# Down-projection of the feed-forward: earlier first operands, a longer last group, sums of weights by DMA

## The chip, the cores and the metric

The kernel runs on one core of a Trainium2 chip. The metric is the device time of one execution in microseconds (us), lower is better; the time of a kernel is the median of its runs.

The engines are TensorE (PE; PEld is its loading of weights), VectorE (DVE), ScalarE (ACT), GpSimd (POOL) and SyncE (SP), which issues most transfers. SBUF is the on-chip memory that all engines read; products of TensorE land in banks of PSUM. Each engine works through its own queue in order and waits there for what others have to deliver.

## What is computed

A trunk of two layers over 512 positions of width 1024, in float32. Each layer is a mixer (attention of three kinds, not touched here), a feed-forward of inner width 2816, and a gated embedding, with layer norms between:

```python
x = layer_norm(alpha * x + mixer(x))
x = layer_norm(alpha * x + swiglu(x, w1, w3, w2))
x = x + sigmoid(x @ w_gate + b_gate) * (p[i] @ w_proj)

def swiglu(x, w1, w3, w2):
    return (jax.nn.silu(x @ w1) * (x @ w3)) @ w2
```

## The kernel before

**Numbers in two parts.** A float32 operand is split into a rounded part (`whi`, `bh`; ScalarE copies it into type fp32r) and the rest (`wlo`, `bl`; VectorE or GpSimd subtracts). `mm3` makes three matmuls of a product: part by rest, part by part, rest by part. `wload` (L137) does it for weights: SyncE loads halves of 128x512 into `wraw` (3 buffers), ScalarE rounds, and a rotation picks the engine for the rest; `DENSE` (L131) gives two of three to VectorE and one to GpSimd. Weight pieces live in 4 buffers `hi` and 4 `lo`.

**The feed-forward** (`swiglu`, L652) has 22 tiles of 128 rows of the inner width. `up` (L656) makes one tile: 8 products by w1 and 8 by w3, in all 48 matmuls of 512 columns (`ps_h`, two banks), then silu on ScalarE and the product on VectorE. The first 16 tiles go in 4 groups of 4 (`GROUPS`). A group's down-projection (`down`, L687) is a product of matrices cut into 2x2 blocks with seven block products in place of eight, on sums and differences of blocks: `B[k][i]` are blocks of the hidden tiles (`halves`, buffers of tag `pl`), `W(j, k)` blocks of w2 (`w2raw`, buffers of tag `qk`, of which there are 3), `n1` to `n4` differences of B, `s3` and `s1` sums of W. `operands(m)` (L715) makes product m's operands and splits them; the loop of L745 asks for those of m+1 and then makes product m with 12 matmuls, 6 for each of two banks `ps_m`. The products are added into x or into four accumulators (`sums`).

**The order.** `down` is a generator with one step for each product. It is made after a group's four `up`s, but nothing of it is issued until it is first asked, which is after the first `up` of the next group; `after_up(2)` then takes two steps after each `up`. Steps of the fourth group lie among the tiles that are left: tiles 16 to 21 (`plain`), which go in pairs. Tile 16 is followed by three steps, tile 17 by the rest and by `flush` (L767), which puts the accumulators into x with six operations of VectorE and three of GpSimd. Pairs are kept as parts in `gT` (a `qk` buffer for each pair) and multiplied by rows of w2 in `down_pair` (L781), 48 matmuls a pair; the last pair is done in `finish`, where the norm and the gate follow tile by tile.

All instructions of the kernel are placed by a planner that simulates the engines: the order of the code is a priority, and what is ready in its simulation may go ahead if buffers are free. The result is one fixed order on each engine.

Of the kernel before, what the change touches and what calls it, by code (L numbers as in the profile page):

```python
# [8 lines left out]
F32 = mybir.dt.float32  # L9
F32R = mybir.dt.float32r  # L10
# [4 lines left out]
P = 128  # L15
LINE = 32
S = 512
# [32 lines left out]
def trunk(ctx: ExitStack, tc: tile.TileContext, a, out):  # L50
# [81 lines left out]
    STICK = (acts, dve), (gps,)  # L132
    MLA = (acts, dve), (gps,)
    FOX = (acts,), (gps,)
    engines, count = [DENSE], [0]

    def wload(src, n, m):  # L137
# [512 lines left out]


    def swiglu(i, finish):  # L652
        w1, w3, w2 = a["ffn_w1"][i], a["ffn_w3"][i], a["ffn_w2"][i]
        nf = DFF // P

        def up(f, g, cuts=1):  # L656
# [30 lines left out]
        def down(f0, halves):  # L687

            first = f0 == 0
            raw = []
            for p in range(2):
                t = quad("w2raw", F32)
                nc.sync.dma_start(t.rearrange("p (k j) c -> p k (j c)", k=2),  # L700
                                  w2[(f0 + 2 * p) * P:(f0 + 2 * p + 2) * P, :].rearrange("(k p) c -> p k c", k=2))
                raw.append(t)
            B = [[halves[i][:, :, k, :] for i in range(2)] for k in range(2)]

            def W(j, k):
                return [t[:, 2 * k + j, :] for t in raw]

            s3, s1 = ([wide(n)[:, q * S:(q + 1) * S] for q in range(2)] for n in ("s3", "s1"))
            n1, n2, n3, n4 = (temp(n).rearrange("p (q s) -> p q s", q=2) for n in ("n1", "n2", "n3", "n4"))

            def add(o, a, b, eng):
                for q in range(2):
                    eng[q].tensor_tensor(o[q], a[q], b[q], ALU.add)

            def operands(m):  # L715
                tt = dve.tensor_tensor
                ws, bs = [(W(0, 1), B[1][0]), (W(0, 0), B[0][0]), (s3, n3), (s1, n1), (s1, n2), (W(1, 1), n4),
                          (s1, B[1][1])][m]
                if m == 2:
                    add(s3, W(0, 0), W(1, 0), (dve, gps))  # L720
                    tt(n3, B[0][1], B[1][1], ALU.subtract)
                elif m == 3:
                    add(s1, W(1, 0), W(1, 1), (dve, gps))
                    tt(n1, B[0][0], B[0][1], ALU.subtract)
                elif m == 4:
                    add(s1, s1, W(0, 0), (dve, gps))
                    dve.scalar_tensor_tensor(n2, B[1][1], -1.0, n1, ALU.mult, ALU.subtract)
                elif m == 5:
                    tt(n4, n2, B[1][0], ALU.add)
                elif m == 6:  # L730
                    add(s1, s1, W(0, 1), (dve, gps))
                parts = act.tile([P, 2, S], F32R, tag="g", bufs=3, name="bparts")
                bh, bl = (parts[:, c, :].rearrange("p (q s) -> p q s", q=2) for c in range(2))
                acts.copy(bh, bs)
                dve.tensor_tensor(bl, bs, bh.bitcast(F32), ALU.subtract)
                hi = wpool.tile([P, D], F32R, tag="hi", name="whi")
                lo = wpool.tile([P, D], F32R, tag="lo", name="wlo")
                wh, wl = ([v[:, q * S:(q + 1) * S] for q in range(2)] for v in (hi, lo))
                for q in range(2):
                    acts.copy(wh[q], ws[q])  # L740
                    (dve, gps)[(q + m) % 2].tensor_tensor(wl[q], ws[q], wh[q].bitcast(F32), ALU.subtract)  # L741
                return (bh, bl), (wh, wl)

            ready = operands(0)
            for m in range(7):  # L745
                (bs, ws), ready = ready, operands(m + 1) if m < 6 else None
                for tb in range(2):
                    ps = (ps_pq, ps_o)[tb]("ps_m")
                    for q in range(2):
                        mm3(ps, both(bs, lambda v: v[:, q, blk(tb)]), both(ws, lambda v: v[q]), q == 0, q == 1)  # L750
                    if m in (0, 5, 6):
                        o = x[tb + 2 * (m == 6)][:, (m == 5) * S:(m == 5) * S + S]
                        if first:
                            dve.scalar_tensor_tensor(o, o, ALPHA, ps, ALU.mult, ALU.add)
                        else:
                            dve.tensor_tensor(o, o, ps, ALU.add)
                    else:
                        if first and tb == 0:
                            sums[m] = row_tile("acc").rearrange("p (t c) -> p t c", t=2)
                        o = sums[m][:, tb, :]  # L760
                        if first:
                            acts.copy(o, ps)
                        else:
                            dve.tensor_tensor(o, o, ps, ALU.add)
                yield

        def flush():  # L767

            q1, q7, p5, p6 = (sums[m] for m in (1, 2, 3, 4))
            h00, h01, h10, h11 = (x_rows[:, 2 * i:2 * i + 2, j * S:(j + 1) * S] for j in range(2) for i in range(2))  # L770
            dve.tensor_tensor(p6, q1, p6, ALU.add)
            gps.tensor_tensor(h00, h00, q1, ALU.add)
            dve.tensor_tensor(h10, h10, q7, ALU.add)
            dve.tensor_tensor(q7, q7, p5, ALU.subtract)
            gps.tensor_tensor(h01, h01, p5, ALU.add)
            dve.scalar_tensor_tensor(h11, h11, ALPHA, q7, ALU.mult, ALU.add)
            dve.tensor_tensor(h10, h10, p6, ALU.subtract)
            gps.tensor_tensor(h01, h01, p6, ALU.add)
            dve.tensor_tensor(h11, h11, p6, ALU.subtract)
# [14 lines left out]
        for f0 in range(0, 4 * GROUPS, 4):  # L794
            halves = [spare("gb").rearrange("p (q k s) -> p q k s", q=2, k=2) for _ in range(2)]
            for n in range(4):
                up(f0 + n, as_block(halves, n // 2, n % 2), 2 if f0 + n == 0 else 1)
                after_up(2)
            after_up(7)
            steps = down(f0, halves)  # L800
        waiting = None
        for f in range(nf - plain, nf, 2):
            group = quad("gT")
            gs = [(group[:, 2 * j, :], group[:, 2 * j + 1, :]) for j in range(2)]
            for j in range(2):
                up(f + j, as_parts(gs[j]))
                if f == nf - plain:
                    after_up(3)
            if waiting is None:
                after_up(7)  # L810
                flush()
            else:
                down_pair(*waiting)
            waiting = (f, gs)
        finish(gs, row_weights(w2, [nf - 2, nf - 1]))


# [295 lines left out]
    for i in range(DEPTH):  # L1113
# [12 lines left out]

        def finish(gs, w):
            first_half, rest = gate(i, e, a["w_gate"][i], done)
            finish_rows(gs, w, False, norm_params("ln2_g", "ln2_b"), after=first_half)
            rest()  # L1130

# [104 lines left out]
```

## Time and profile before

| | |
|---|---|
| median of 3 runs | 1392.12 us (1392.1 to 1394.07) |
| the profiled execution | 1396.08 us |
| its span, first to last instruction | 1394.4 us |
| PE busy | 1346.4 us, 97% |
| DVE, ACT, POOL busy | 925.9, 659.9, 534.1 us |
| mean granted TensorE clock | 0.986 |
| moved by DMA | 131.74 MB, mean 94 GB/s |

The profile is of one execution. A row of the view by line groups instructions of one line, engine and operation; the number behind the bar `|` is the busy time of the group and the mean time of one, then the idle time of that engine just ahead of them and what ended it. A row in order of time has the start, the time taken (of several merged ones, from the first to the last end), and in brackets the idle time ahead of it and what ended that. `out<-in` are the program's names. Matmuls are pipelined: one takes longer than the distance to the next, so their pace is read from the starts. In the feed-forward the first layer's stage lies from some 286 to 640 us, the second's from 975 to 1330.

### The profile page before, as it was taken

Reading aid. Unit: us, or ns where it says so; the run is one execution under the profiler, and the core shown is the slowest. Engines: PE = TensorE matmul, PEld = TensorE weight load, DVE = VectorE, ACT = ScalarE, POOL = GpSimd, SP = SyncE. Lnnn points to the kernel's source line nnn. Section 1 sums busy time; section 2 is a strip of 40 time slices with the busy share of each in tenths; the row PEclk is TensorE's granted clock in tenths of the full one; section 3 lists DMA queues with packets and bytes.
Section 4 is the critical chain, followed back from the end, with each engine's and each line's share of the span. In section 5 each row is a group of like instructions: output and inputs, shape, how many; then the busy total and the mean of one; then the engine's idle time right before and its main releaser. Section 6 shows DMA issues by size and latency. Waiting matters only on the chain.

```text
span 1394.4 us, 18865 instructions
## 1 busy us (share of the span) xinstructions
PE 1346.4 (97%) x6680; PEld 1126.1 (81%) x6680; DVE 925.9 (66%) x1600; ACT 659.9 (47%) x1362; POOL 534.1 (38%) x479
## 2 busy tenths in 40 slices
PE   7999999799999998999989999998999999989998
PEld 7888787588888887887879888876888888868887
DVE  4656778753757656948755775798346668578495
ACT  4556767552433333423455665754434334243252
POOL 5655733122334324612235554442224334255131
PEclk9999999999999999999999999999999999999999
DMA  6211321241323132232234221123413131403312
GB/s 230 89 44 47 112 66 62 90 159 61 121 83 102 58 115 89 101 105 75 73 111 131 98 91 62 61 99 105 143 56 135 54 121 44 167 32 129 98 61 98
DMA packets 64303, 131.74 MB, mean 94 GB/s; under 512 B 7361, under 2 KB 8129, under 8 KB 64193
## 3 DMA queue, kind: packets, MB, share of 16 engines
q1 hardware_dynamic: 61440, 120.74, 25.6%
q0 software_dynamic: 2768, 9.80, 2.1%
q8 instruction: 52, 0.85, 0.3%
q14 instruction: 43, 0.34, 0.1%
HBM read 127.80 MB, written 2.72 MB: 94 GB/s over the span
## 4 chain that ended last, share of the span: by engine, by line
PE 84%; DVE 9%; ACT 3%; DMA 2%; issue 2%; POOL 0%; SPq 0%; DVEq 0%; ACTq 0%; POOLq 0%
PE ps_h L154 11%; PE ps_h L153 11%; PE ps_h L152 11%; PE ps_m L152 4%; PE ps_m L153 4%; PE ps_m L154 4%; PE ps_qkT L152 3%; PE ps_qkT L153 3%; PE ps_qkT L154 3%; PE ps_y L152 2%; PE ps_o L406 2%; PE ps_y L153 2%; PE ps_y L154 2%; PE ps_g L152 2%; PE ps_g L154 2%; PE ps_g L153 2%
## 5 line engine op out<-in xcount | busy, mean ns | idle before, releaser
L148 POOL TENSOR_TENSOR wlo<-wraw,whi 128x512 fp32r<-128x512 f32 (+2 forms) x191 | 255.3, 1346 | 453.5 <-ACT whi L147 402.3
L147 ACT CAST whi<-wraw 128x512 fp32r<-128x512 f32 (+1 forms) x338 | 200.1, 616 | 323.3 <-DMA wraw<-in_ffn_w_dram 83.6
L152 PE MATMUL ps_h<-xTl,whi 128*128 128x512 f32 (+1 forms) x736 | 279.8, 380 | 0.0
L153 PE MATMUL ps_h<-xTh,whi 128*128 128x512 f32 (+1 forms) x736 | 279.6, 380 | 0.0
L154 PE MATMUL ps_h<-xTh,wlo 128*128 128x512 f32 (+1 forms) x736 | 279.5, 380 | 0.0
L148 DVE TENSOR_TENSOR wlo<-wraw,whi 128x512 fp32r<-128x512 f32 (+1 forms) x172 | 141.9, 837 | 92.9 <-ACT whi L147 90.5
L153 PEld LDWEIGHTS ps_h<-xTh,whi 128*128 128x128 f32 x736 | 138.4, 188 | 26.5
L152 PEld LDWEIGHTS ps_h<-xTl,whi 128*128 128x128 f32 x736 | 138.4, 188 | 26.2
L154 PEld LDWEIGHTS ps_h<-xTh,wlo 128*128 128x128 f32 x736 | 138.4, 188 | 26.1
L152 PE MATMUL ps_m<-wlo,bparts 128*128 128x512 f32 x224 | 89.4, 399 | 9.4 <-DVE wlo L741 8.9
L153 PE MATMUL ps_m<-whi,bparts 128*128 128x512 f32 x224 | 88.8, 396 | 0.0
L154 PE MATMUL ps_m<-whi,bparts 128*128 128x512 f32 x224 | 88.5, 395 | 0.0
L152 PE MATMUL ps_qkT<-xTl,whi 128*128 128x512 f32 x192 | 78.5, 409 | 2.4 <-DVE qkT L331 1.0
L154 PE MATMUL ps_qkT<-xTh,wlo 128*128 128x512 f32 x192 | 78.0, 406 | 0.0
L153 PE MATMUL ps_qkT<-xTh,whi 128*128 128x512 f32 x192 | 77.5, 404 | 0.0
L740 ACT CAST whi<-s 128x512 fp32r<-128x512 f32 x64 | 36.9, 619 | 85.4 <-PE ps_h L153 49.6
L741 POOL TENSOR_TENSOR wlo<-s,whi 128x512 fp32r<-128x512 f32 x32 | 42.8, 1340 | 76.3 <-ACT whi L740 76.3
L741 POOL TENSOR_TENSOR wlo<-w2raw,whi 128x512 fp32r<-128x512 f32 x24 | 34.6, 1440 | 91.9 <-ACT whi L740 83.3
L152 PE MATMUL ps_v<-wlo,xTh 128*128 128x256 f32 (+1 forms) x192 | 56.3, 294 | 6.8 <-ACT neg_tri L109 6.4
L682 DVE TENSOR_TENSOR gb<-silu,ps_h 128x256 f32<-128x256 f32 x64 | 24.0, 416 | 57.5 <-PE ps_h L154 53.7
L152 PEld LDWEIGHTS ps_m<-wlo,bparts 128*128 128x128 f32 x224 | 42.9, 192 | 20.0 <-DVE wlo L741 9.7
L210 DVE TENSOR_TENSOR x<-x,ps_y 128x512 f32<-128x512 f32 x64 | 43.0, 679 | 22.9 <-PE ps_y L154 22.6
(274 smaller groups left out, 3216.1 us busy)
## 6 DMA issues: line engine op xcount, KB each, us to landing
wraw<-in_ffn_w_dram SPq DMA_DIRECT2D x200, 256.0 KB, 2.7
w2raw<-in_ffn_w_dram SPq DMA_DIRECT2D x16, 1024.0 KB, 6.4
wraw<-in_w_gate_dram SPq DMA_DIRECT2D x32, 256.0 KB, 2.6
wraw<-in_w_qkf_dram SPq DMA_DIRECT2D x32, 256.0 KB, 2.6
wraw<-in_w_qkb_dram SPq DMA_DIRECT2D x16, 256.0 KB, 2.9
wraw<-in_a_w_out_dram SPq DMA_DIRECT2D x16, 256.0 KB, 2.6
kbias<-nd_dram POOLq DMA_DIRECT2D x8, 512.0 KB, 4.8
wraw<-in_c_w_out_dram SPq DMA_DIRECT2D x16, 256.0 KB, 2.6
```

The lines of the kernel that those rows point to most:

```text
L147: (eng_hi.copy if eng_hi is acts else eng_hi.tensor_copy)(hi[:, c:end], raw)
L148: eng_lo.tensor_tensor(lo[:, c:end], raw, hi[:, c:end].bitcast(F32), ALU.subtract)
L152: nc.tensor.matmul(o, lhsT=lhs[0], rhs=rhs[1], start=first, stop=False)
L153: nc.tensor.matmul(o, lhsT=lhs[0], rhs=rhs[0], start=False, stop=False)
L154: nc.tensor.matmul(o, lhsT=lhs[1], rhs=rhs[0], start=False, stop=last)
L210: nc.vector.tensor_tensor(xs, xs, ps, ALU.add)
L406: nc.tensor.matmul(o_ps[:, kb * P:], lhsT=val[:, c:c + 2 * HD], rhs=t, start=first and n == 0, stop=last and n == 1, skip_group_check=True)
L682: nc.vector.tensor_tensor(half[:, p, k, :], s[:, fs], h[:, fs], ALU.mult)
L740: acts.copy(wh[q], ws[q])
L741: (dve, gps)[(q + m) % 2].tensor_tensor(wl[q], ws[q], wh[q].bitcast(F32), ALU.subtract)
```

## The change

- The rests of the feed-forward's weights are all made on VectorE (`SWIGLU`), and so are those of the down-projection's operands; the gate's layers and later take `DENSE` again.
- The sums of w2's blocks, which VectorE and GpSimd made (L713), are made by transfers on GpSimd's queue: one copies a block, others add a block to what is there. Two each make `s3` and the first `s1` at a group's start; a fifth is issued after the operands of product 3, a sixth after those of product 4. Block `W(1, 0)`, which appears in sums only, is not loaded any more.
- The blocks are cut otherwise: `k` runs over pairs of tiles, so that `B[0]` needs only the first two tiles of a group. Products 0 and 1 change places; the first takes `W(0, 0)` and `B[0][0]`.
- `down` gets one more `yield` after `operands(0)`, and `next(steps)` asks for it at once: w2's transfers, four sums and the first operands stand in the code ahead of the next `up`.
- The last group's steps go two after each of tiles 16 to 19, and `flush` after tile 19. Tiles 16 and 17 are kept in `pl` buffers, 18 to 21 in two `qk` buffers. The first pair is multiplied after tile 20, the second after tile 21.

```diff
--- before.py
+++ after.py
@@ -132,6 +132,7 @@
     STICK = (acts, dve), (gps,)
     MLA = (acts, dve), (gps,)
     FOX = (acts,), (gps,)
+    SWIGLU = (acts,), (dve,)
     engines, count = [DENSE], [0]
 
     def wload(src, n, m):
@@ -651,6 +652,7 @@
 
     def swiglu(i, finish):
         w1, w3, w2 = a["ffn_w1"][i], a["ffn_w3"][i], a["ffn_w2"][i]
+        engines[0] = SWIGLU
         nf = DFF // P
 
         def up(f, g, cuts=1):
@@ -694,41 +696,42 @@
 
 
             first = f0 == 0
+            blocks = w2[f0 * P:(f0 + 4) * P, :].rearrange("(k q p) (j c) -> p q k j c", q=2, k=2, j=2)
             raw = []
             for p in range(2):
                 t = quad("w2raw", F32)
-                nc.sync.dma_start(t.rearrange("p (k j) c -> p k (j c)", k=2),
-                                  w2[(f0 + 2 * p) * P:(f0 + 2 * p + 2) * P, :].rearrange("(k p) c -> p k c", k=2))
+                nc.sync.dma_start(t[:, 0, :], blocks[:, p, 0, 0, :])
+                nc.sync.dma_start(t[:, 2:4, :], blocks[:, p, 1])
                 raw.append(t)
             B = [[halves[i][:, :, k, :] for i in range(2)] for k in range(2)]
 
             def W(j, k):
                 return [t[:, 2 * k + j, :] for t in raw]
 
-            s3, s1 = ([wide(n)[:, q * S:(q + 1) * S] for q in range(2)] for n in ("s3", "s1"))
+            wsum = [wide(n)[:, 0:D].rearrange("p (q c) -> p q c", q=2) for n in ("s3", "s1")]
+            s3, s1 = ([t[:, q, :] for q in range(2)] for t in wsum)
+
+            def add(t, k, j, first=False):
+                gps.dma_start(t, blocks[:, :, k, j, :], accum_op=ALU.bypass if first else ALU.add)
+
+            add(wsum[0], 0, 0, True)
+            add(wsum[0], 0, 1)
+            add(wsum[1], 0, 1, True)
+            add(wsum[1], 1, 1)
             n1, n2, n3, n4 = (temp(n).rearrange("p (q s) -> p q s", q=2) for n in ("n1", "n2", "n3", "n4"))
-
-            def add(o, a, b, eng):
-                for q in range(2):
-                    eng[q].tensor_tensor(o[q], a[q], b[q], ALU.add)
 
             def operands(m):
                 tt = dve.tensor_tensor
-                ws, bs = [(W(0, 1), B[1][0]), (W(0, 0), B[0][0]), (s3, n3), (s1, n1), (s1, n2), (W(1, 1), n4),
+                ws, bs = [(W(0, 0), B[0][0]), (W(0, 1), B[1][0]), (s3, n3), (s1, n1), (s1, n2), (W(1, 1), n4),
                           (s1, B[1][1])][m]
                 if m == 2:
-                    add(s3, W(0, 0), W(1, 0), (dve, gps))
                     tt(n3, B[0][1], B[1][1], ALU.subtract)
                 elif m == 3:
-                    add(s1, W(1, 0), W(1, 1), (dve, gps))
                     tt(n1, B[0][0], B[0][1], ALU.subtract)
                 elif m == 4:
-                    add(s1, s1, W(0, 0), (dve, gps))
                     dve.scalar_tensor_tensor(n2, B[1][1], -1.0, n1, ALU.mult, ALU.subtract)
                 elif m == 5:
                     tt(n4, n2, B[1][0], ALU.add)
-                elif m == 6:
-                    add(s1, s1, W(0, 1), (dve, gps))
                 parts = act.tile([P, 2, S], F32R, tag="g", bufs=3, name="bparts")
                 bh, bl = (parts[:, c, :].rearrange("p (q s) -> p q s", q=2) for c in range(2))
                 acts.copy(bh, bs)
@@ -738,17 +741,22 @@
                 wh, wl = ([v[:, q * S:(q + 1) * S] for q in range(2)] for v in (hi, lo))
                 for q in range(2):
                     acts.copy(wh[q], ws[q])
-                    (dve, gps)[(q + m) % 2].tensor_tensor(wl[q], ws[q], wh[q].bitcast(F32), ALU.subtract)
+                    dve.tensor_tensor(wl[q], ws[q], wh[q].bitcast(F32), ALU.subtract)
+                if m == 3:
+                    add(wsum[1], 0, 0)
+                elif m == 4:
+                    add(wsum[1], 1, 0)
                 return (bh, bl), (wh, wl)
 
             ready = operands(0)
+            yield
             for m in range(7):
                 (bs, ws), ready = ready, operands(m + 1) if m < 6 else None
                 for tb in range(2):
                     ps = (ps_pq, ps_o)[tb]("ps_m")
                     for q in range(2):
                         mm3(ps, both(bs, lambda v: v[:, q, blk(tb)]), both(ws, lambda v: v[q]), q == 0, q == 1)
-                    if m in (0, 5, 6):
+                    if m in (1, 5, 6):
                         o = x[tb + 2 * (m == 6)][:, (m == 5) * S:(m == 5) * S + S]
                         if first:
                             dve.scalar_tensor_tensor(o, o, ALPHA, ps, ALU.mult, ALU.add)
@@ -766,7 +774,7 @@
 
         def flush():
 
-            q1, q7, p5, p6 = (sums[m] for m in (1, 2, 3, 4))
+            q1, q7, p5, p6 = (sums[m] for m in (0, 2, 3, 4))
             h00, h01, h10, h11 = (x_rows[:, 2 * i:2 * i + 2, j * S:(j + 1) * S] for j in range(2) for i in range(2))
             dve.tensor_tensor(p6, q1, p6, ALU.add)
             gps.tensor_tensor(h00, h00, q1, ALU.add)
@@ -794,24 +802,29 @@
         for f0 in range(0, 4 * GROUPS, 4):
             halves = [spare("gb").rearrange("p (q k s) -> p q k s", q=2, k=2) for _ in range(2)]
             for n in range(4):
-                up(f0 + n, as_block(halves, n // 2, n % 2), 2 if f0 + n == 0 else 1)
+                up(f0 + n, as_block(halves, n % 2, n // 2), 2 if f0 + n == 0 else 1)
                 after_up(2)
             after_up(7)
             steps = down(f0, halves)
-        waiting = None
-        for f in range(nf - plain, nf, 2):
-            group = quad("gT")
-            gs = [(group[:, 2 * j, :], group[:, 2 * j + 1, :]) for j in range(2)]
-            for j in range(2):
-                up(f + j, as_parts(gs[j]))
-                if f == nf - plain:
-                    after_up(3)
-            if waiting is None:
+            next(steps)
+        waiting = []
+        for f in range(nf - plain, nf):
+            if len(waiting) < 2:
+                g = spare("gT", F32R).rearrange("p (c s) -> p c s", c=2)
+            elif f % 2 == 0:
+                group = quad("gT")
+            if len(waiting) >= 2:
+                g = group[:, 2 * (f % 2):2 * (f % 2) + 2]
+            up(f, as_parts((g[:, 0, :], g[:, 1, :])))
+            waiting.append((g[:, 0, :], g[:, 1, :]))
+            after_up(2)
+            if f == nf - plain + 3:
                 after_up(7)
                 flush()
-            else:
-                down_pair(*waiting)
-            waiting = (f, gs)
+            if f >= nf - 2:
+                n = 2 * (f - nf + 2)
+                down_pair(nf - plain + n, waiting[n:n + 2])
+        gs = waiting[-2:]
         finish(gs, row_weights(w2, [nf - 2, nf - 1]))
 
 
@@ -1126,6 +1139,7 @@
 
         def finish(gs, w):
             first_half, rest = gate(i, e, a["w_gate"][i], done)
+            engines[0] = DENSE
             finish_rows(gs, w, False, norm_params("ln2_g", "ln2_b"), after=first_half)
             rest()
```

## Rows read from the trace of the kernel before

**Rows 1.** page, part 1: busy us (share of the span) and instructions of each engine

```profile
PE 1346.4 (97%) x6680; PEld 1126.1 (81%) x6680; DVE 925.9 (66%) x1600; ACT 659.9 (47%) x1362; POOL 534.1 (38%) x479
```

**Rows 2.** stages: span, engines' busy us (instructions), granted clock, DMA share, GB/s

```profile
400.00:450.00 50.00, 50.00 (x222) 41.38 (x222) 38.58 (x48) 18.42 (x33) 20.06 (x15) 1.00 0.23 78
...
530.00:560.00 30.00, 25.57 (x103) 20.49 (x102) 21.97 (x22) 11.77 (x21) 16.21 (x11) 0.89 0.10 33
...
1225.00:1245.00 20.00, 15.04 (x58) 11.58 (x57) 15.96 (x17) 8.27 (x15) 12.51 (x8) 0.91 0.08 26
```

**Rows 3.** TensorE in order of time: start, us, instruction, idle before

```profile
535.83 0.39 PE L153 MATMUL ps_h<-xTh,whi 128*128 128x512 f32 x1
536.06 0.39 PE L154 MATMUL ps_h<-xTh,wlo 128*128 128x512 f32 x1
540.88 0.80 PE L152 MATMUL ps_m<-wlo,bparts 128*128 128x512 f32 x1 [4.43 <-DVE wlo L741]
541.47 0.63 PE L153 MATMUL ps_m<-whi,bparts 128*128 128x512 f32 x1
541.89 0.63 PE L154 MATMUL ps_m<-whi,bparts 128*128 128x512 f32 x1
```

**Rows 4.** TensorE in order of time, at the same place of the second layer

```profile
1231.17 0.50 PE L152 MATMUL ps_m<-wlo,bparts 128*128 128x512 f32 x1 [4.43 <-DVE wlo L741]
```

**Rows 5.** chain that ended last, in order of time: start, us, what

```profile
536.48 0.70 DVE silu L673
...
537.21 0.63 ACT gT L124
...
537.86 0.69 DVE gT L125
538.55 0.60 DVE s L713
539.15 1.68 DVE wlo L741
```

**Rows 6.** ScalarE in order of time, ahead of that product

```profile
531.04 0.60 ACT L667 ACTIVATE silu<-ps_h 128x512 f32<-128x512 f32 x1 [6.49 <-PE ps_h L154]
...
537.73 1.13 ACT L740 CAST whi<-w2raw 128x512 fp32r<-128x512 f32 x2
```

**Rows 7.** SyncE's queue in order of time, merged: start, us over which issued

```profile
445.39 76.29 SPq L144 DMA_DIRECT2D wraw<-in_ffn_w_dram  x24
521.73 0.94 SPq L700 DMA_DIRECT2D w2raw<-in_ffn_w_dram  x2
```

**Rows 8.** by line, first feed-forward: x count, busy, mean ns, idle before

```profile
L148 DVE TENSOR_TENSOR wlo<-wraw,whi 128x512 fp32r<-128x512 f32 x64 | 50.3, 797 | 38.9 <-ACT whi L147 38.4
L148 POOL TENSOR_TENSOR wlo<-wraw,whi 128x512 fp32r<-128x512 f32 x32 | 45.4, 1418 | 131.2 <-ACT whi L147 128.3 <-DVE wlo L148 2.9
...
L713 DVE TENSOR_TENSOR s<-w2raw 128x512 f32<-128x512 f32 x8 | 12.4, 1555 | 0.2
...
L776 DVE SCALAR_TENSOR_TENSOR x<-x,acc 128x1024 f32<-128x1024 f32 x1 | 3.4, 3406 | 0.0
```

**Rows 9.** line L741, whole span: duration ns min/median/max

```profile
L741 DVE TENSOR_TENSOR wlo<-s,whi x32: 678/693/2300, 343.8 to 1255.7; 128x512 fp32r<-128x512 f32 x32
```

**Rows 10.** DMA issues: count, KB each, median us to landing

```profile
w2raw<-in_ffn_w_dram SPq DMA_DIRECT2D x16, 1024.0 KB, 6.4
...
ln_g<-in_ln_g_dram POOLq DMA_DIRECT2D x4, 512.0 KB, 4.0
```

**Rows 11.** VectorE in order of time, ahead of the first feed-forward stage

```profile
270.84 1.80 DVE L199 SCALAR_TENSOR_TENSOR x<-ln,rstd,ln_b 128x768 f32<-128x768 f32 x1
272.56 1.21 DVE L148 TENSOR_TENSOR wlo<-wraw,whi 128x512 fp32r<-128x512 f32 x1
...
286.51 1.02 DVE L199 SCALAR_TENSOR_TENSOR x<-ln,rstd,ln_b 128x768 f32<-128x768 f32 x1
```

**Rows 12.** TensorE in order of time, in that stretch

```profile
272.79 1.94 PE L177 MATMUL ps_xt<-identr,x 128*128 128x128 f32 x8 [2.09 <-DVE x L199]
```

## The prediction

> **What bounds the kernel now.** I read the page's busy shares first: TensorE is busy for 97% of the span, so nothing but TensorE's own gaps and slow stretches can be won [rows 1]. Next came the busy times by stage, to find them: in the feed-forward stages TensorE is busy in all 50 of 50 us at a granted clock of 1.00, with VectorE at 38.58 and GpSimd at 20.06 [rows 2]. The stage stands at its floor there, and freeing VectorE or GpSimd in such a stretch is worth nothing. Each of the two layers has one exception: 25.57 of 30 us at clock 0.89 in the first, 15.04 of 20 at 0.91 in the second [rows 2]. TensorE in order of time shows what it is: the first product of the fourth (last) group of the down-projection waits, 4.43 us idle in the one layer and 4.43 in the other [rows 3, 4]. The chain of waits names what ended last: after the up-projection of tile 16 come the product with the gate, its two parts, then the sum of weights for the third product (L713) and the rounding rest of the first product's weights, 1.68 us, all in a row on VectorE and ScalarE [rows 5].
>
> Why there and in no other group? ScalarE's first rounding of w2 for that group stands at 537.73, behind the roundings of tile 16's result, after ScalarE had been idle for 6.49 us and again until 537.21 [rows 5, 6]. SyncE's queue has the two transfers of that group's w2 at 521.73, behind 24 weight pieces of up-projections whose issue stretches over 76 us [rows 7]. The order on the engines is a planner's, with the order of the code as its priority. The code puts the start of `down(f0, ...)` after the next up-projection, because the generator begins only when it is first asked; and the last group has its third buffer of tag `qk` taken by `gT` of tile 16, so both w2 tiles wait for the group before.
>
> **The change part by part, against the profiled execution** (1396.08 us with a span of 1394.4; the median of the runs is 1392.12, 4.0 below, and I carry the same difference over).
>
> *The stall of the last group, removed: -14.2.* Starts 536.06 and 540.88 lie 4.82 apart where two neighbours lie 0.23 apart: 4.59 lost. After it the matmuls start 0.42 to 0.43 apart (541.47 to 541.89), which is the 1.2 GHz level where 0.23 is the 2.4 GHz level [rows 3]; ten such steps cost 0.20 each, the first step of 0.59 costs 0.36, and the last two 0.15: 2.5. That is 7.1 a layer. A second way bounds it: idle 4.43 plus 30 x 0.11 of clock is 7.7, in the other layer 4.96 plus 20 x 0.09 is 6.8 [rows 2]; the first counts some low clock in the idle time twice. I take 7.1 for each, 14.2 for both. Does the change reach the cause? `next(steps)` puts the w2 transfers and the first operands ahead of tile 16's pieces on SyncE, ScalarE and VectorE; the first operand now needs only the first two tiles of its group (`n % 2, n // 2`), and tiles 16 and 17 take `pl` buffers, so that the third `qk` buffer is free for w2. A w2 transfer lands after 6.4 us [rows 10], and it would be issued a whole up-projection (48 matmuls at 0.23, 10.9 us) before its use. I count the full 14.2, ending at nothing left; the lower end is half of it, one layer's worth.
>
> *What is passed by the moved step.* Its w2 transfers go ahead of the next tile's pieces on SyncE: four of at most 512 KB in place of two of 1024 KB. Its two weight roundings take one of four `whi` buffers ahead of the next up-projection, whose second piece then starts loading when the tile before ends; that piece is needed 24 matmuls (5.4 us) after, and a load takes a rounding of 0.6 and a rest of 0.69 for each half [rows 6, 9]. Nothing on the path.
>
> *GpSimd to VectorE.* In the first layer's stage 32 + 28 rounding rests leave GpSimd (32 at a mean of 1418 ns stand in [rows 8]; the 28 are half of L741's) for VectorE, at 0.69 when GpSimd is still [rows 9]: 60 x 0.69 = +41. The 16 half-sums of L713 leave VectorE: 8 at 1555 ns [rows 8] and 8 like them, -25. VectorE's own operations beside GpSimd get shorter: 64 at a mean of 797 [rows 8] against 689 to 693 when undisturbed [rows 9], -7, and the others of the stage by the same reading some -20. VectorE ends about 10 us lower in 350, off the path either way [rows 2]: 0.
>
> *At both ends of the stage VectorE is on the path.* While the norms ahead of the stage run, TensorE waits 2.09 us for L199 [rows 12], and L199 takes 1.80 beside GpSimd where it takes 1.02 alone, and a rest of the first tiles' weights 1.21 where 0.69 would do [rows 11, 9]. The change takes two rests off GpSimd in that stretch and puts them on VectorE: from -1.30 (contention gone, the two behind the path) to +1.38 (two more in it, contention from the norm's own GpSimd steps staying). The same trade comes at the end of the stage with the gate's weights, so there are four such stretches. Nearest to the rows is a small gain; I take -0.15 each, -0.6, with ends of 4 x -1.30 = -5.2 and 4 x 1.38 = +5.5.
>
> *Sums by DMA.* Six transfers of 512 KB a group on GpSimd's queue, four of them adding to what lies in SBUF. No row has an adding transfer. Below, it costs what a 512 KB transfer of this queue takes, 4.0 us; above, a transfer that reads both summands, 1024 KB, 6.4 [rows 10], and half as much again because it must also wait in line with w1 and w3: some 9. The third product's sum is issued at the group's start, far ahead. The fifth and the seventh each follow the last reading of the sum before: from there to their own matmuls lie one product (12 x 0.23 = 2.7) and an up-projection (10.9), 13.6, less the two roundings and rests of some 2, leaves 11.6. So 0, with cover of 2.6 us over the upper end. The GpSimd queue waits in order, but until the flush nothing else is on it.
>
> *The last group over four up-projections.* Its operations get twice the cover. The flush has one up-projection behind it instead of two before tile 16's row product: VectorE's six steps, up to 3.41 us beside GpSimd [rows 8], need between 7 and 14 us. Four of them depend only on products up to the fifth, so they run beside the sixth and the seventh: 0, at worst 2 a layer.
>
> The sum: -14.2 - 0.6 = -14.8. Profiled 1381.3, median **1377.3**.
>
> **The rivals.** *A, as above:* from 1371.5 (1392.1 less 2 x 7.7 and 5.2) to 1383.4 (less 14.2, plus 5.5). *B, the wait is only cut:* the last group still waits for part of its operands, or the flush comes late, so that half of the gain stays: 1385, between 1381 and 1389, a flush that comes 2 us late in each layer among them. For it: four `whi` buffers are all taken at that point; against it: in three groups of four the same buffers suffice without a gap. *C, the wait moves:* the first product is there, but a later one of the last group (the second layer already shows one more wait in its chain, behind L764) takes its place in full: 1392, within 1389 to 1395. *D, the sums come late:* ScalarE's rounding of the sum is in order, so while it waits for an adding transfer the roundings of w1 and w3 are queued behind it, and TensorE waits for those. The fifth and seventh products of 4 groups in 2 layers make 16 waits; each costs what the transfer takes above 11.6 us. At 12.5 us the 14.8 are used up, at 14 us the loss is 38 and the time 1416. It decides from about twice the 6.4 us of a 1024 KB transfer.
>
> The Trainium skill bears on D in two places. Its page "Collectives: The Full Stack" (section "The bandwidth ceiling") has a reducing transfer read two sources on one ring, at about half a copy's rate (1.93); by that the 4.0 us would be an estimated 7.7, and the sum stays. Its page "SBUF — State Buffer" (section "Who interferes with whom") speaks against the move to GpSimd's queue: its descriptors wait while VectorE runs in a two-port mode. It excepts additions and subtractions of two tensors, which the rows of this stage's VectorE are. No run here shows either yet.
>
> **How the numbers follow.** A 0.64, B 0.16, C 0.08, D 0.12. The likeliest gives 1377.3. A and B make 0.80, so the range goes from A's lower end, 1371.5, to B's upper end, 1389. About 0.2% (2.8 us) is what a measurement of this kernel can tell from no change: faster 0.80, same 0.08, slower 0.12.
>
> **What would show it.** Right: TensorE without idle time between tile 15 and the row products, its starts 0.23 apart, granted clock 1.00 there; w2's first rounding for the last group before tile 16 ends; no 1.2 us forms of VectorE inside the stage; adding transfers landing within 9 us. Wrong: waits of ScalarE for a sum that last longer than 8 us with TensorE idle behind them (D); TensorE idle at the first row product (B, flush) or at a later product of the last group (C); longer waits of TensorE for L199 than 2.09 us (the ends of the stage).

## The result and the profile after

The changed kernel's median is 1380.24 us (four runs, 1377.74 to 1380.63) against 1392.11 us, 11.9 us less. The ratio over all runs, which is not the quotient of the two medians, is 0.9909 with a 95% interval of 0.9891 to 0.9926 (15.2 to 10.3 us). The forecast was 1377.3, within 1371.5 to 1389. The profiled execution of after took 1380.52 us, 0.3 above its median; that of before stood 4.0 above its own.

Part 1 and part 6 of the page of after: busy time of each engine, and the transfers (KB each, median us to landing).

```profile
PE 1339.6 (97%) x6680; PEld 1122.4 (81%) x6680; DVE 882.7 (64%) x1696; ACT 656.9 (48%) x1362; POOL 351.9 (26%) x367
...
s<-in_ffn_w_dram POOLq DMA_DIRECT2D x48, 512.0 KB, 5.8
w2raw<-in_ffn_w_dram SPq DMA_DIRECT2D x16, 512.0 KB, 4.2
```

TensorE is as busy as before [rows 1], in a shorter span. GpSimd lost 182 us of work and VectorE 43, and none of that is what made the time. The windows of after that answer to [rows 2]: TensorE is busy in all of both, at full clock, where it was 25.57 of 30 and 15.04 of 20.

```profile
530.00:560.00 30.00, 30.00 (x134) 24.85 (x133) 19.10 (x29) 11.15 (x20) 5.27 (x3) 1.00 0.27 62
1225.00:1245.00 20.00, 20.00 (x90) 16.55 (x89) 13.10 (x19) 7.03 (x14) 5.27 (x3) 1.00 0.49 113
```

Another stretch got worse. TensorE in order of time ahead of the first feed-forward, where before had 2.09 [rows 12], and VectorE there:

```profile
275.05 1.94 PE L178 MATMUL ps_xt<-identr,x 128*128 128x128 f32 x8 [6.08 <-DVE x L200]
```

```profile
270.71 1.28 DVE L196 SCALAR_TENSOR_TENSOR ln<-x,neg_mean,ln_g 128x1024 f32<-128x1024 f32 x1 [4.03 <-DMA ln_g<-in_ln_g_dram]
```

VectorE waits 4.03 us for the norm's parameter `ln_g`. GpSimd's queue of after in order of time shows why that is late:

```profile
253.75 0.81 POOL L715 DMA_DIRECT2D s<-in_ffn_w_dram  x1 [12.72 <-ACT prob L469]
255.97 0.73 POOL L715 DMA_DIRECT2D s<-in_ffn_w_dram  x1 [1.41 <-ACT pth L124]
258.77 1.25 POOL L715 DMA_DIRECT2D s<-in_ffn_w_dram  x1 [2.08 <-DMA s<-in_ffn_w_dram]
262.30 1.21 POOL L715 DMA_DIRECT2D s<-in_ffn_w_dram  x1 [2.27 <-DMA s<-in_ffn_w_dram]
263.04 1.05 POOL L183 DMA_DIRECT2D ln_g<-in_ln_g_dram  x1
```

The first group's sums were placed ahead of the load of `ln_g`, and an adding transfer waits on the queue until the one before it has landed; so `ln_g` is issued at 263.04 and lands at 270.62, after 7.58 us by the chain of waits. In before the same queue issued it 20 us earlier:

```profile
242.65 0.59 POOL L182 DMA_DIRECT2D ln_g<-in_ln_g_dram  x1
```

In the second layer of after `ln_g` stands ahead of the sums on that queue (924.40 against 930.27), and there the stretch is no longer than before.

The two traces side by side, by the starts of TensorE's matmuls. From the first `ps_h` to the last `ps_y` a layer takes 6.93 and 6.98 us less; from there to the last `ps_g` (the gate) 1.72 and 0.98 less; the norms ahead of the feed-forward (last `ps_o` to first `ps_h`) 3.28 more in the first layer and 0.39 less in the second. That makes 13.7 us less. The other 1.9 of the 15.6 between the two profiled executions lie in stretches that the change doesn't touch, 1.7 of them ahead of the first layer's norms. That place (the last `ps_o`) lies between 259.0 and 261.5 us in the profiles of all kernels here, and 1.8 apart in two executions of one kernel, so this part is no gain of the change.

### The profile page after: what moved, and what is told of

It is laid out like the page before. It is cut to its first block, busy times and chain, and to the rows that moved or that the text cites. A ratio compares the mean times of both kernels' runs of the same rounds, so it can differ in the third digit from the quotient of the medians.

```text
span 1378.8 us, 18770 instructions
## 1 busy us (share of the span) xinstructions
PE 1339.6 (97%) x6680; PEld 1122.4 (81%) x6680; DVE 882.7 (64%) x1696; ACT 656.9 (48%) x1362; POOL 351.9 (26%) x367
## 4 chain that ended last, share of the span: by engine, by line
PE 88%; DVE 6%; DMA 2%; ACT 2%; issue 1%; POOL 0%; SPq 0%; DVEq 0%; ACTq 0%; POOLq 0%
PE ps_h L155 12%; PE ps_h L154 12%; PE ps_h L153 12%; PE ps_m L155 4%; PE ps_m L154 4%; PE ps_m L153 4%; PE ps_qkT L153 3%; PE ps_qkT L154 3%; PE ps_qkT L155 3%; PE ps_y L153 3%; PE ps_y L154 3%; PE ps_y L155 3%; PE ps_o L407 2%; PE ps_g L153 2%; PE ps_g L155 2%; PE ps_g L154 2%
## 5 line engine op out<-in xcount | busy, mean ns | idle before, releaser
L148 ACT CAST whi<-wraw 128x512 fp32r<-128x512 f32 (+1 forms) x338 | 199.0, 616 | 357.3 <-PE ps_h L154 104.8
L149 DVE TENSOR_TENSOR wlo<-wraw,whi 128x512 fp32r<-128x512 f32 (+1 forms) x244 | 175.5, 741 | 100.4 <-ACT whi L148 100.1
L149 POOL TENSOR_TENSOR wlo<-wraw,whi 128x512 fp32r<-128x512 f32 (+2 forms) x119 | 155.0, 1315 | 169.3 <-ACT whi L148 132.4
L715 POOL DMA_DIRECT2D s<-in_ffn_w_dram x48 | 50.8, 1059 | 440.0 <-DVE wlo L744 362.4
L744 DVE TENSOR_TENSOR wlo<-s,whi 128x512 fp32r<-128x512 f32 x64 | 45.7, 756 | 66.5 <-ACT whi L743 66.5
L154 PE MATMUL ps_m<-whi,bparts 128*128 128x512 f32 x224 | 87.1, 389 | 0.0
L155 PE MATMUL ps_m<-whi,bparts 128*128 128x512 f32 x224 | 87.1, 389 | 0.0
L154 PE MATMUL ps_v<-whi,xTh 128*128 128x256 f32 (+1 forms) x192 | 56.0, 292 | 0.0
```

Source lines behind the costliest of these rows:

```text
L148: (eng_hi.copy if eng_hi is acts else eng_hi.tensor_copy)(hi[:, c:end], raw)
L149: eng_lo.tensor_tensor(lo[:, c:end], raw, hi[:, c:end].bitcast(F32), ALU.subtract)
L154: nc.tensor.matmul(o, lhsT=lhs[0], rhs=rhs[0], start=False, stop=False)
L155: nc.tensor.matmul(o, lhsT=lhs[1], rhs=rhs[0], start=False, stop=last)
L715: gps.dma_start(t, blocks[:, :, k, j, :], accum_op=ALU.bypass if first else ALU.add)
L744: dve.tensor_tensor(wl[q], ws[q], wh[q].bitcast(F32), ALU.subtract)
```

## The experiments

The table has each kernel's median (one run where no interval is given), the two lengths from the start of a layer's first `ps_h` to the start of its last `ps_g` (feed-forward with gate), and TensorE's idle time ahead of the first norm's transposes (the row of 6.08 above), all in us. The kernel before ran again beside each set of runs: at 1394.09 beside the norm's loads, no early start and the last group over two tiles, at 1392.68 beside the others. So medians of different sets can lie 1 to 2 us apart for that reason alone, and the ratios, each against its own set, are the better comparison.

| kernel | median | ratio, interval | layer 1 | layer 2 | idle at first norm |
|---|---|---|---|---|---|
| before | 1392.11 | | 413.00 | 412.51 | 2.09 |
| after | 1380.24 | 0.9909, 0.9891 to 0.9926 | 404.35 | 404.55 | 6.08 |
| norm's loads on SyncE | 1377.18 | 0.9888, 0.9871 to 0.9904 | 404.86 | 404.73 | 2.47 |
| no early start | 1379.85 | | 404.60 | 404.14 | 6.53 |
| last group over two tiles | 1380.86 | | 404.43 | 404.18 | 6.11 |
| sums on the engines | 1378.10 | 0.9885, 0.9868 to 0.9902 | 404.79 | 404.32 | 2.40 |
| GpSimd's rests back | 1381.02 | 0.9922, 0.9900 to 0.9945 | 405.06 | 404.78 | 4.92 |
| before, early start only | 1378.89 | | 405.29 | 405.19 | 2.09 |
| before, `pl` buffers only | 1378.26 | 0.9896, 0.9880 to 0.9911 | 405.80 | 405.32 | 2.11 |
| after, both ends undone | 1393.56 | | 410.40 | 411.98 | 5.54 |

**The loss at the first norm: the norm's loads on SyncE.**

```diff
-        nc.gpsimd.dma_start(t, vec.rearrange(
+        nc.sync.dma_start(t, vec.rearrange(
```

> The changed kernel with the norms' gains and biases (and the gate's bias) loaded by SyncE's queue in place of GpSimd's. Theory: in the changed kernel the gain of the first norm is issued on GpSimd's queue only after an adding transfer there has waited for the copy before it, and TensorE idles 6.08 us for L200 where it idled 2.09 before; on SyncE's queue the wait is gone, the idle time falls back to some 2 us, the first feed-forward starts 3.3 us earlier and the median falls from 1380.2 to about 1377. Rival: the idle time is VectorE's, which now makes all four rests of weights in that stretch; then L200 comes as late as now and the median stays within 1 us of 1380.2. Second rival: SyncE's own queue is held by weight pieces waiting for buffers, the gain comes later still, and the time is over 1381.

The idle time is back near before's, with nothing else of the change touched. TensorE in order of time:

```profile
271.07 1.40 PE L178 MATMUL ps_xt<-identr,x 128*128 128x128 f32 x8 [2.47 <-DVE x L200]
```

The queue behind the waiting sums is the cause of the 3.3 to 3.6 us. The median moved by 3.1, as it should; the two kernels' intervals overlap, so the trace is the proof, not the median.

**Is it the early start?** The extra `yield` and `next(steps)` taken out of the changed kernel:

```diff
             ready = operands(0)
-            yield
...
             steps = down(f0, halves)
-            next(steps)
```

> The changed kernel without the early start: w2's transfers, the four sums and the first operands of a group stand in the code after the next up-projection again; the last group still goes over four up-projections and its tiles 16 and 17 still lie in pl buffers. Theory that the order is what removed the stall: TensorE idles again ahead of the first product of the last group, some 4.4 us in each layer, with some 2.5 us of low clock after it, and the profiled span grows from 1378.8 to about 1393. Rival, that the third qk buffer and the longer last group are enough: no idle time there, span within 2 us of 1378.8.

No stall came back: TensorE is busy for 30.00 of 30 us from 530 on and for 20.00 of 20 from 1225 on.

```profile
530.00:560.00 30.00, 30.00 (x134) 24.86 (x133) 19.02 (x28) 11.15 (x20) 5.27 (x3) 1.00 0.25 56
```

The place of the group's start in the code, which the prediction named first, was not needed.

**Is it the longer last group?**

```diff
-            after_up(2)
-            if f == nf - plain + 3:
+            after_up(3)
+            if f == nf - plain + 1:
```

> The changed kernel with the last group's steps over two up-projections as before (three after tile 16, the rest and the flush after tile 17), with the early start kept. Theory that the early start removed the stall: no idle time of TensorE from the first up-projection to the last row product, span within 2 us of 1378.8. Rival, that spreading did: TensorE idles ahead of the first product or of a later one of the last group, 4 to 7 us a layer, span 1387 to 1393.

No stall either, in both windows. Each edit alone seemed unnecessary, so what both kernels still had in common was looked for: tiles 16 and 17 in `pl` buffers, which leaves the third `qk` buffer to w2.

**The buffer alone, in the kernel before.** Nothing else of the change is in it:

```diff
-            group = quad("gT")
-            gs = [(group[:, 2 * j, :], group[:, 2 * j + 1, :]) for j in range(2)]
+            if waiting is None:
+                pair = [spare("gT", F32R).rearrange("p (c s) -> p c s", c=2) for _ in range(2)]
+                gs = [(t[:, 0, :], t[:, 1, :]) for t in pair]
+            else:
+                group = quad("gT")
+                gs = [(group[:, 2 * j, :], group[:, 2 * j + 1, :]) for j in range(2)]
```

> The kernel before with one thing of the change: the parts of tiles 16 and 17 lie in pl buffers instead of a qk buffer; order of the code, two up-projections for the last group, sums on the engines, GpSimd's rests all as before. Theory 'buffer': one of the two w2 tiles of the last group is loaded as early as in the groups before (which start in the same order of code and have no gap), ScalarE rounds w2 ahead of tile 16's parts, no stall, about 1378. Rival 'order of the code' (my prediction named it first: the start of the group stands behind the next up-projection): the stall stays, 7.1 a layer, about 1392.

The order of the code is before's, and both stalls are gone. SyncE's w2 transfers of this kernel, in order of time: the second tile of the third group and the first of the last go out together, the last one 62 us later, all ahead of the 521.73 of [rows 7]. ScalarE rounds the last group's w2 at 519.47, where it was 537.73 [rows 6], and TensorE's first product follows tile 16 at once.

```profile
432.51 0.89 SPq L700 DMA_DIRECT2D w2raw<-in_ffn_w_dram  x2
...
495.07 0.38 SPq L700 DMA_DIRECT2D w2raw<-in_ffn_w_dram  x1
```

```profile
519.47 1.14 ACT L740 CAST whi<-w2raw 128x512 fp32r<-128x512 f32 x2 [2.85 <-issue]
```

```profile
532.82 0.39 PE L154 MATMUL ps_h<-xTh,wlo 128*128 128x512 f32 x1
533.05 0.39 PE L152 MATMUL ps_m<-wlo,bparts 128*128 128x512 f32 x1
```

That single run took 1377.71 us. The same kernel, run more often to compare this one part with the whole change:

> The kernel before with tiles 16 and 17 in pl buffers and nothing else: measured to see how much of the change's gain this one part has. Theory 'the buffer is all that was needed': 2 x 7.1 = 14.2 of gain, 1377.5 to 1379, ratio 0.990, no worse than the whole change. Rival 'the other parts gain too': 1383 or more.

It gains 14.4 us of 1392.68, as much as the whole change or more; its interval overlaps that of after. From the first `ps_h` to the last `ps_y` a layer takes 357.3 us, against 357.6 in after and 364.5 in before, so nothing else of the change gains in that stretch. What else tells this kernel from after lies at the first norms (24.34 against 28.67 us, with 25.39 in before) and at the gate (48.49 and 47.98 against 46.79 and 47.00).

**The early start alone, in the kernel before.** The reverse of the second experiment.

```diff
             ready = operands(0)
+            yield
...
             steps = down(f0, halves)
+            next(steps)
```

> The kernel before with one thing of the change: the extra yield after the first operands and the call that asks for them at once, so the last group's two w2 buffers are claimed ahead of tile 16's gT. Theory 'buffer' (the stall is the third qk buffer going to tile 16's gT, so that both w2 tiles wait for the group before): the first w2 transfer of the last group is issued some 60 us earlier than 521.7, both stalls of 7.1 are gone, 1392.1 - 14 = about 1378, and the fixed loss at the first norms that the changed kernel has (3.3) is absent. Rival 'the buffer is only short elsewhere': gT of tile 16 now waits for a qk buffer, VectorE's product for tile 16 comes late, TensorE idles by 2 to 5 us at tile 17 or at the first row products, 1385 to 1392.

Both stalls are gone here too: asked for early, w2 takes the third `qk` buffer ahead of tile 16's `gT` (its transfers at 436.00 and 498.12), and TensorE has no gap later in the stage either, so `gT` had its buffer in time. So the change removes the cause twice over: by either of two parts w2 gets that buffer.

**Both undone, in the changed kernel.** No early start, and before's loop for the last tiles: the last group over two of them, `gT` in `qk`. The new cut of the blocks, the sums by DMA and VectorE's rests stay.

> The changed kernel with both the early start and the spread last group undone, and gT of tiles 16 and 17 back in a qk buffer; the new cut of the blocks, the sums by DMA and VectorE's rests stay. Theory 'buffer': w2 of the last group waits for the group before again, the first product of the last group stalls in both layers, 4 to 7 us each: 1388 to 1394. Rival 'the new cut or the load taken off GpSimd would do' (the first product needs only the first two tiles, and less w2 is loaded): no stall, about 1380.

The stall is back in both layers. SyncE's w2 transfers and TensorE, in order of time:

```profile
523.56 0.43 SPq L703 DMA_DIRECT2D w2raw<-in_ffn_w_dram  x1
...
524.98 0.43 SPq L704 DMA_DIRECT2D w2raw<-in_ffn_w_dram  x1
```

```profile
540.15 0.50 PE L153 MATMUL ps_m<-wlo,bparts 128*128 128x512 f32 x1 [2.76 <-DVE wlo L744]
```

It is 2.76 us idle in each layer in place of 4.43 [rows 3, 4], so the other parts shorten the wait but don't remove it. The feed-forward with the gate is 6.0 and 7.4 us longer than in after. Of that 4.4 and 5.6 are there by the 1600th matmul of the stage, idle time and slower pace behind it, against some 6.9 for the stall of before. The other 1.7 and 1.8 come later, with TensorE idle for 0.8 and 1.3 us more at the gate. So it is chance that 1393.56 is so near the time of before.

**Sums on the engines.** VectorE and GpSimd add halves again, and block `W(1, 0)` is loaded again; all else is the changed kernel. It ran once, in 1375.77 us, and then more often:

```diff
-            add(wsum[0], 0, 0, True)
-            add(wsum[0], 0, 1)
-            add(wsum[1], 0, 1, True)
-            add(wsum[1], 1, 1)
...
+                    add(s3, W(0, 0), W(1, 0))
...
+                    add(s1, W(1, 0), W(1, 1))
```

> The changed kernel with the sums of w2's blocks made by VectorE and GpSimd again, and all of w2 loaded (1 MB in two pieces a tile), everything else as changed. Theory: the sums are worth nothing inside the stage, where TensorE is at its floor either way (6.9 us below before's in each layer), and without the adding transfers ahead of the first norm's gain the first feed-forward starts some 3.3 us earlier: span about 1375.5. Rival: the transfers are what frees VectorE in time, and without them TensorE idles inside the stage: span 1381 or more.

> The changed kernel with the sums of weights made by VectorE and GpSimd again (half each, as before the change), block W(1, 0) loaded again, all else of the change kept: measured to tell it from the changed kernel's 1380.2. Theory: its gain over the changed kernel is the 3.3 us at the first norms, and nothing in the stage: 1375.5 to 1377, ratio to the kernel before 0.988. Rival (the one look was a low one): 1380, ratio 0.991.

VectorE then works for 225.59 us of the 350 between 290 and 640, against 201.19 in after, and TensorE is busy for all 350 in both. Moving the sums to DMA is worth nothing in the stage and costs 3.3 to 3.6 us at the first norm. 1378.10 is below both kernels' medians but 1.1 above the 1375.5 to 1377 that was expected; from after it isn't separated.

**GpSimd's rests back**, for the weights and for every second half of the operands, with the sums still by DMA.

```diff
-        engines[0] = SWIGLU
...
-                    dve.tensor_tensor(wl[q], ws[q], wh[q].bitcast(F32), ALU.subtract)
+                    (dve, gps)[(q + m) % 2].tensor_tensor(wl[q], ws[q], wh[q].bitcast(F32), ALU.subtract)
```

> The changed kernel with GpSimd's rounding rests back (the feed-forward's and the gate's weights, and every second half of the operands), sums still by DMA on GpSimd's queue. Theory 'beside the path': in the stage nothing changes, and what GpSimd's rests cost lies at the gate (1.7 in the first layer, 1.0 in the second, as the kernel before lost there): 1380.2 + 2.7 = about 1383. Rival 'rests behind waiting sums': GpSimd issues in order, so a rest stands behind a sum that waits for the transfer before it (up to 8.7 us landing) and TensorE idles inside the stage: 1390 or more. Rival 'GpSimd costs nothing anywhere': 1380.

TensorE has no gap in the stage, so rests behind waiting sums were covered. At the gate it waits 0.29 and 0.22 us for L200, where before waited 1.28 and 0.92 and after does not wait: GpSimd's rests explain some 0.5 of those 2.2 us, not the 2.7 that was expected. Where the rest of the gate's gain comes from stays open, and part of it may be chance: in the two profiles of the kernel with `pl` buffers only, the first layer's wait for that line is 0.40 in one and 1.28 in the other. The median is 0.8 above after's, within the interval.

**How late may a sum be?** The fifth and sixth transfers of sums are issued twice, then four times in a row (their blocks are counted so many times):

```diff
                 if m == 3:
-                    add(wsum[1], 0, 0)
+                    for _ in range(2):
+                        add(wsum[1], 0, 0)
                 elif m == 4:
-                    add(wsum[1], 1, 0)
+                    for _ in range(2):
+                        add(wsum[1], 1, 0)
```

> The changed kernel with the fifth and the sixth transfer of sums of each group issued twice in a row (these two blocks are counted twice in the sums). Each adding transfer waits for the one before on the same sum, so the sum is ready after T = 2 x 5.8 = 11.6 us instead of 5.8. The prediction's formula, 16 x (T - 11.6): 0, about 1380. Rival from the trace after (product 4's rounding of the sum stands 8.8 us behind the issue of the fifth transfer, product 6's 18.8 behind that of the sixth, and TensorE has rounded pieces of w1 and w3 in store): ScalarE waits some 3 us at 8 places, TensorE does not: 1380. Rival 'no slack': 8 x 3 = 24 us, 1404.

> The same two transfers issued four times in a row (their blocks are counted four times): T = 4 x 5.8 = 23 us. The prediction's formula, 16 x (T - 11.6): +186, about 1566. From the trace after: only the fifth transfer's 8 waits are late, by 23 - 8.8 = 14 less the pieces that TensorE has in store (up to one up-projection, 10.9): 8 x (3.5 to 14) = 28 to 115, 1408 to 1495; the sixth's 18.8 are passed by 4, which the store covers. Rival 'a late sum costs nothing': 1380.

They took 1446.44 and 1607.42 us, 66 and 227 more than after, and all the expected times were too low. ScalarE in order of time with the transfers doubled: it waits 8.74 us for the sum of the seventh product, and `bparts` of the sixth product stand behind it. TensorE then waits for those:

```profile
391.06 1.14 ACT L743 CAST whi<-s 128x512 fp32r<-128x512 f32 x2 [8.74 <-DMA s<-in_ffn_w_dram]
...
392.59 0.61 ACT L737 CAST bparts<-n 128x512 fp32r<-128x512 f32 x1
```

```profile
393.25 0.79 PE L153 MATMUL ps_m<-wlo,bparts 128*128 128x512 f32 x1 [4.79 <-ACT bparts L737]
393.84 0.63 PE L154 MATMUL ps_m<-whi,bparts 128*128 128x512 f32 x1
394.27 0.63 PE L155 MATMUL ps_m<-whi,bparts 128*128 128x512 f32 x1
```

The sum was ready T = 17.06 us after its first transfer's issue at 374.00, not 11.6: the two landed after 7.4 and 9.3 us. T less the idle time gives the cover: 17.06 - 4.79 = 12.3. After the wait the matmuls start 0.43 apart, as after the stall of before [rows 3]. From the first `ps_h` to the last `ps_y` the two layers take 65.6 us longer than in after: 42.6 of idle time, and 23 of that slower pace.

With four transfers, the fifth's T is 24.16 to 24.70 in the first layer's four groups, and TensorE waits 12.12 to 13.78; the first of them:

```profile
383.24 0.79 PE L153 MATMUL ps_m<-wlo,bparts 128*128 128x512 f32 x1 [12.12 <-DVE wlo L744]
```

By the means, 24.3 - 12.8 = 11.5 of cover for the fifth. For the sixth 27.2 - 10.9 = 16.3, behind a group already late. I had expected from the trace of after that TensorE's stored pieces would hide the doubled sums; they don't, because a product's own parts stand in ScalarE's queue behind the late sum. The eight waits of the first layer add up to 94.5 us and those of the second to 96.8, so 191.3 of the 227 are idle time. The mean granted clock fell from 0.991 to 0.928: nearly all of the other 36 is the slower pace after the waits, some 34 by the starts of the matmuls.

## Why the prediction was right or wrong, point by point

- **The stall, -14.2.** Right in size: 6.93 and 6.98 a layer against 7.1. Of the two causes that it gave side by side, the runs keep one. The third `qk` buffer is the cause, since that alone frees the stall in before. The place of the start in the code is a cause only in so far as it decides who gets that buffer; in the kernel without early start it changed nothing. The groups before the last, which start in the same place without a gap, could have told that in advance.
- **w2's transfers and `whi` buffers, 0.** Right: no gap of TensorE between the start of the stage and the gate, in either layer.
- **GpSimd to VectorE, 0 in the stage.** Right. VectorE was to end some 10 us a layer lower; it fell by 15.2, from 216.36 to 201.19 us, in the first layer's 350, and by 9.6 in the second's 345.
- **The four norm stretches, -0.6.** The sum was +3.3 - 1.7 - 0.4 - 1.0 = +0.2, inside the ends, but by luck: a loss and three gains that were not foreseen in these sizes cancel. The first stretch failed, by another mechanism than VectorE's rests. The step at fault is "until the flush nothing else is on it": GpSimd's queue also carries `ln_g` and `ln_b` of the norm ahead. The prediction counted that the sums wait in order, and not what stood behind them. The gate's two stretches gained 2.7 where 0.3 was forecast.
- **Sums by DMA, 0.** Right in the stage. Landings of all 48 transfers of sums in after, in us, were within the upper end of 9, and the shortest a little under the lower end of 4.0. (6.4 and half as much again is 9.6 and not 9, which leaves 2.0 of cover over it and not 2.6.)

```profile
DMA to landing us min/median/max: 3.7/5.8/8.7
```

- **Cover of 11.6 us, and rival D.** The cover was well sized (11.5 measured for the fifth), and D's mechanism is real: ScalarE already waits in after for eight sums, 24.1 us in all and 3.9 at the longest, and TensorE doesn't. Its price was too low: with the transfers doubled, T was 11.85 to 13.6 for the fifth and 14.2 to 17.1 for the sixth, on which the formula gives about 41 us (8 x 0.6 + 8 x 4.5), and 66 were lost. The waits are priced about right in sum, at 42.6 us of idle time, though not one by one: 12 at the fifth sums and 31 at the sixth. What the formula leaves out is TensorE's slower pace after each wait, which the prediction did count for the stall (2.5 us); here it cost 23, and the granted clock fell from 0.991 to 0.980. The page "Collectives: The Full Stack" (The bandwidth ceiling) of the Trainium skill has a reducing transfer at about half a copy's rate, by which the prediction's estimate was 7.7 us; it says this of rings between ranks. The trace agrees in part: the 16 copies of after land after a median of 3.9 us and the 32 adding transfers after 5.9, 1.5 times as long, with 8.7 as the longest. The page "SBUF — State Buffer" (Who interferes with whom) of the Trainium skill has GpSimd's descriptors wait while VectorE runs in a two-port mode, and excepts operations on two tensors. Of VectorE's 324 instructions between 290 and 640 us in after, 300 are of the excepted kind, and all eight fifth sums were rounded 5.79 to 5.98 us after their issue: this fits the exception, and the warning itself is not shown by any run here.
- **The flush, 0.** Right, with two tiles as with four: no gap of TensorE there.
- **From the profile to the median.** The step that failed here is the carried 4.0. The profiled sum, 1381.3, was only 0.8 too high, in part by luck: the stretches at the norms and the gate nearly cancelled, and 1.9 of the difference lie where nothing was touched. The median was 2.9 above 1377.3, because after's profiled execution stands 0.3 above its median and not 4.0. The 3.3 of the first norm alone is as large as the miss: without it the changed kernel runs at 1377.18, in a set where before took 1394.09.

## What to carry to other kernels

When one round of a loop stalls and the rounds like it don't, compare what they hold, not only their order: here the last group lost one buffer to a neighbour, and giving it that buffer back brings what the whole change brings. Work that is moved to a DMA queue has to be followed through that queue to every transfer behind it, also those of the stage before. Work taken off an engine that is not on the path (15 us off VectorE and 84 off GpSimd in the first layer's stage) gains nothing there: before with `pl` buffers only keeps that work and passes the stage in the same time. And a wait of TensorE costs more than its idle time: with the sums late, 23 us of slower pace came on top of 42.6.

## What the runs showed of the hardware

Of the 512 KB transfers of sums in after, the 16 that copy landed after 3.7 to 6.5 us, median 3.9, and the 32 that add after 5.6 to 8.7, median 5.9. Their issue holds GpSimd for 0.73 to 1.29 us. Two on the same buffer in a row take the sum of their landings, and the landings themselves can be longer: with the transfers doubled, 7.4 and 9.3 us in the sixth's place, where the fifth's two of the same group took 5.8 and 5.8. The load of `ln_g`, 512 KB, took 5.8 us in before and 7.6 in after, where it was issued within a microsecond of a sum.
